# Sums of squares and low halves of weights on VectorE, and squares added beside the first up products, in a two-layer transformer kernel

## Chip, cores and metric

One Trainium2 chip, one core. The metric is device time in microseconds of one execution; the figure for the kernel before is the median of 3 runs. Engines are named TensorE (PE, with PEld for its weight loads), VectorE (DVE), ScalarE (ACT), GpSimd (POOL) and SyncE (SP).

## What is computed

Two layers over 512 tokens of width 1024 in float32. Each layer normalises its input, projects it (`w_in`), runs three groups of four attention heads (a forgetting one, a differential one with two maps a head, and a latent one), adds the output projection, normalises again and adds a feed-forward block with a causal convolution over three tokens:

```python
for i in range(DEPTH):
    h = rmsnorm(x, ln1_g[i]) @ w_in[i]
    ...
    x = x + jnp.concatenate([o_fox, o_diff, o_mla], axis=-1) @ w_o[i]
    up = causal_dwconv(rmsnorm(x, ln2_g[i]) @ w_up[i], conv_w[i], conv_b[i])
    g, u = up[..., :D_FF], up[..., D_FF:]
    x = x + (jax.nn.silu(g) * u) @ w_down[i]
return rmsnorm(x, final_g)
```

`rmsnorm(x, g)` is `x * rsqrt(mean(x * x) + 1e-6) * g`, the mean over the 1024 features of a token.

## The kernel before, in words

The residual lies transposed in eight tiles `x[0]` to `x[7]` (128 features by 512 tokens, float32; in the order listings `x_94` to `x_101`). Every operand of a product is split into a high half, the value rounded to fp32r, and a low half, the rest, and each product of two operands is three TensorE instructions (`mm3`): high by high, high by low, low by high. For an operand made on the chip (`split`; tiles named `a`), ScalarE writes the high half and VectorE the low one. For weights, `weights` hands out the next piece of a fixed list and keeps two pieces cut ahead: a load into one of three buffers `raw` on SyncE's queue, the high half `whi` by ScalarE, the low half `wlo` by VectorE, with four buffers of each. One kind is an exception (`ahead`): for the second piece of each of the 15 projection tiles of `w_fm` in a layer, GpSimd makes the low half.

A norm is not applied before its product. `Norm.halves` splits x times the gain, the product runs on that, and 1/rms is multiplied in behind it. The sum over features needs the squares: `Norm.square` has ScalarE square a tile and GpSimd add it to the tile `r` (seven sums for eight tiles). `Norm.sums` then lets TensorE sum over partitions (products with a column of ones), VectorE scales (`vn`), GpSimd takes the root (`rsn`), and `Norm.spread` spreads it over partitions by TensorE and copies it to `rb` by ScalarE.

The order of the work in a layer:

- Start: products with `w_fx`, tokens on the rows, in eight steps, one per x tile, of twelve products with 292 columns each. `Norm.ready` makes the halves and squares just ahead of each step, where they were not made by the layer before. In layer 0 all of this waits for the loads.
- The first two projection tiles (`fm`), during which the sums and 1/rms are made, then the values `w_dv`.
- The woven part: a planner (`Plan`, `weave`) counts times with its own costs per engine and decides when a step of the two heads in work goes next and when a filler (a projection tile, latent products, the output projection) goes instead. Its costs for a low half differ between VectorE and GpSimd, so the engine chosen changes the order.
- The rest of the output projection (`w_o2`): for each of eight x tiles six products, the sum into x on VectorE, the halves for the next norm, and its square.
- `ffn`: 22 pairs of up products (ft, gu), each 24 products of 512 columns; for each, VectorE multiplies by 1/rms (`u`), ScalarE and VectorE do the convolution (`w`), and a pair gives one tile of the hidden layer. In the first half eleven pairs are followed by eight down products, then the second half.

PSUM has three banks `mm` for products, two `sc` for scores, two `at` for transposes and sums, and one `o` for head outputs. In `ffn` the first up product (0, 0) goes before the sums, (0, 1) comes behind them with the spreading after its fourth step, and then VectorE begins with (0, 0).

An instruction's place on its engine is fixed when the program is built; it is mostly the order of the code, but an instruction that would wait can be passed by a later one. In the profile nearly every instruction has line 133 (the helper that the planner calls), and loads have 276, so rows are told apart by tile names.

Of the kernel before, what the change touches and what calls it, by code (L numbers as in the profile page):

```python
# [8 lines left out]
F32 = mybir.dt.float32  # L9
F32R = mybir.dt.float32r  # L10
AF = mybir.ActivationFunctionType
ALU = mybir.AluOpType
# [164 lines left out]
def build(tc, xT, cst, par, lamv, w_fm, w_dv, w_fx, w_uq, w_ukv, w_o, w_o2, w_up, w_dn, w_dt, fin, out):  # L177
# [4 lines left out]
    with ctx:  # L182
# [61 lines left out]
        def col(l, o, j=0):  # L244
            k = l * PL + o + j
            return par_sb[:, k:k + 1]
# [39 lines left out]
        def ahead():  # L286

            while state["cut"] < min(len(pieces), state["use"] + CUT_AHEAD):
                i, off, w = pieces[state["cut"]]
                while state["load"] < min(len(chunks), i + 3):  # L290
                    load()
                src = raws[i][:, off:off + w]
                if chunks[i][0].tensor.name == w_dt.tensor.name:
                    hi, lo = A(), A()
                else:
                    hi, lo = (plan.tile(v, CUT_BUFS, lp.tile([P, S], F32R, name=v, tag=v, bufs=CUT_BUFS))[:, :w] for v in ("whi", "wlo"))
                nc.scalar.activation(hi, src, AF.Copy)
                eng = nc.gpsimd if off and chunks[i][0].tensor.name == w_fm.tensor.name else nc.vector
                eng.tensor_tensor(out=lo, in0=src, in1=hi.bitcast(F32), op=ALU.subtract)
                ready.append((hi, lo))  # L300
                state["cut"] += 1

# [51 lines left out]
        class Norm:  # L354
# [5 lines left out]
            def halves(self, j):  # L360
                self.xs.append(split(x[j], scale=self.g(j)))

            def square(self, eng=None):
                j = self.squares
                self.squares += 1
                sq = R() if j == 0 else W()
                nc.scalar.activation(sq, x[j], AF.Square)
                if j == 0:
                    self.acc = sq
                else:  # L370
                    (eng or nc.gpsimd).tensor_tensor(out=self.acc, in0=self.acc, in1=sq, op=ALU.add)

            def ready(self, k):

                while len(self.xs) <= min(k, KD - 1):
                    self.halves(len(self.xs))
                    if len(self.xs) > 2:
                        self.square()

            def sums(self):  # L380
                while self.squares < KD:
                    self.square()
                self.rs = inv_rms(self.acc, D, "n")

            def spread(self):
# [139 lines left out]
        def attention(l, norm):  # L525
# [385 lines left out]
            for j in range(KD):  # L911
                ps = mm_ps()
                if j % 2 == 0:
                    hi, lo = weights(S, w_o2)
                for k in range(2):
                    c = slice((j % 2 * 2 + k) * P, (j % 2 * 2 + k + 1) * P)
                    mm3(ps, (hi[:, c], lo[:, c]), oT[6 + k], k == 0, k == 1)
                nc.vector.tensor_tensor(out=x[j], in0=ps, in1=x[j], op=ALU.add)
                nxt.halves(j)
                nxt.square()  # L920
            return nxt

        def ffn(l, norm):
            last = l == DEPTH - 1
            nxt = None if last else Norm(lambda j: col(l + 1, O_LN1, j))
            for half in range(2):
                hT = []
                for ft in range(half * HALF, (half + 1) * HALF):
                    y2, tiles = [], []

                    def raw(ps):
                        for k in range(KD):
                            if k % 4 == 0:
                                hi, lo = weights(S, w_up)
                            c = slice(k % 4 * P, (k % 4 + 1) * P)
                            mm3(ps, (hi[:, c], lo[:, c]), norm.xs[k], k == 0, k == KD - 1)
                            if ft == 0 and k == 3 and len(tiles) == 2:
                                norm.spread()

                    for gu in range(2):  # L940
                        if len(tiles) == gu:
                            tiles.append(mm_ps())
                            raw(tiles[-1])
                        if norm.rb is None:
                            norm.sums()
                            tiles.append(mm_ps())
                            raw(tiles[-1])
                        ps = tiles[gu]
                        a = U()
                        nc.vector.tensor_tensor(out=a, in0=ps, in1=norm.rb, op=ALU.mult)  # L950
                        y = W()
                        ch = gu * NFT + ft
                        nc.scalar.activation(y, a, AF.Identity, scale=col(l, O_CW, 88 + ch), bias=col(l, O_CB, ch))
                        for s_, o in ((1, 44), (2, 0)):
                            nc.vector.scalar_tensor_tensor(out=y[:, s_:], in0=a[:, :S - s_], scalar=col(l, O_CW, o + ch), in1=y[:, s_:], op0=ALU.mult, op1=ALU.add)
                        y2.append(y)
                    g, u = y2
                    nc.scalar.activation(g, g, AF.Silu)
                    nc.vector.tensor_tensor(out=u, in0=u, in1=g, op=ALU.mult)
                    hT.append(split(u, lo_eng=nc.gpsimd))  # L960
# [114 lines left out]
```

## Time and profile before

| what | us |
|---|---|
| median of 3 runs (1241.84 to 1244.34) | 1241.91 |
| the profiled execution | 1244.5 |
| its span, first to last instruction | 1242.7 |
| TensorE busy | 1210.6 |
| VectorE busy | 815.0 |
| ScalarE busy | 665.0 |
| GpSimd busy | 288.4 |

Busy times overlap. Products are pipelined: a row gives each some 0.39 us, while with 512 columns one starts about 0.2263 us after the other, so the distance of starts tells the rate. A number in brackets behind a row is the idle time of the engine before it and what ended it. A row with x3 is three instructions merged, with the time from the first's start to the last's end.

### The profile page before, as it was taken

To read this page: it belongs to the slowest core of one execution; us is meant where nothing else is said; L and a number is where in the kernel's file an instruction comes from. 1 tells how busy PE (TensorE), PEld (TensorE's weight loads), DVE (VectorE), ACT (ScalarE), POOL (GpSimd) and SP (SyncE) were. 2 spreads that over 40 slices of the span, in tenths; PEclk is the share of its full clock that TensorE was granted. 3 is DMA by queue.
4 is the path that set the end of the run, shared out by engine and by line. 5 is a ranking of instruction groups with operands and counts; after the bars stand their busy time and mean duration, and the time that the engine had idled before them with its cause. 6 is when DMAs were issued, how large, how long until landed. Compare 5 with 4: busy or idle time off the path is not lost.

```text
span 1242.7 us, 16525 instructions
## 1 busy us (share of the span) xinstructions
PE 1210.6 (97%) x5792; PEld 1010.2 (81%) x5792; DVE 815.0 (66%) x1632; ACT 665.0 (54%) x1323; POOL 288.4 (23%) x378
## 2 busy tenths in 40 slices
PE   6999999999999999999999999999999999999997
PEld 6878877878888888888898788788788888888886
DVE  5578778687665357665554887887767643666743
ACT  5477777565543245444454776875545422454524
POOL 4165353141110001111123636322211100011102
PEclk8999999999999999999999999999999999999999
DMA  5211110222222332223232111113222233222231
GB/s 208 94 68 69 56 51 26 95 78 95 99 92 83 98 119 102 86 86 94 86 115 82 69 65 44 48 38 102 86 102 98 68 101 124 87 100 102 86 118 68
DMA packets 34356, 108.33 MB, mean 87 GB/s; under 512 B 3808, under 2 KB 3936, under 8 KB 34272
## 3 DMA queue, kind: packets, MB, share of 16 engines
q1 hardware_dynamic: 33984, 106.81, 25.8%
q8 instruction: 45, 0.74, 0.2%
q10 hardware_dynamic: 288, 0.47, 0.1%
q14 instruction: 39, 0.32, 0.1%
HBM read 105.16 MB, written 2.10 MB: 86 GB/s over the span
## 4 chain that ended last, share of the span: by engine, by line
PE 86%; DVE 6%; POOL 3%; ACT 2%; issue 2%; DMA 0%; POOLq 0%; DVEq 0%; ACTq 0%
PE mm L133 75%; PE sc L133 5%; PE at L133 4%; DVE a L133 2%; PE o L133 2%; POOL rq L133 1%; POOL wlo L133 1%; DVE row L133 1%; DVE wlo L133 1%; DVE w L133 1%; ACT a L133 1%; DVE x L133 1%; POOL row L133 1%; ACT row L133 0%; ACT u L133 0%
## 5 line engine op out<-in xcount | busy, mean ns | idle before, releaser
L133 PE MATMUL mm<-a,whi 128*128 128x512 f32 x2800 | 872.5, 392 | 4.4 <-DVE a L133 4.4
L133 PEld LDWEIGHTS mm<-a,whi 128*128 128x128 f32 x2800 | 520.7, 188 | 108.7 <-DVE a L133 5.8
L133 PE MATMUL mm<-a,wlo 128*128 128x512 f32 x1400 | 546.1, 390 | 0.0
L133 ACT ACTIVATE whi<-raw 128x512 fp32r<-128x512 f32 (+3 forms) x426 | 248.9, 585 | 373.2 <-PE mm L133 323.9
L133 DVE TENSOR_TENSOR wlo<-raw,whi 128x512 fp32r<-128x512 f32 (+3 forms) x396 | 260.6, 660 | 132.2 <-ACT whi L133 127.2
L133 PEld LDWEIGHTS mm<-a,wlo 128*128 128x128 f32 x1400 | 262.9, 188 | 54.4
L133 POOL TENSOR_TENSOR a<-w,a 128x512 fp32r<-128x512 f32 x44 | 57.2, 1300 | 540.6 <-ACT a L133 521.4
L133 DVE SCALAR_TENSOR_TENSOR w<-u,par_sb,w 128x511 f32<-128x511 f32 (+1 forms) x176 | 132.1, 750 | 32.0 <-ACT w L133 28.9
L133 DVE TENSOR_TENSOR u<-mm,r 128x512 f32<-128x512 f32 x88 | 60.9, 692 | 107.3 <-PE mm L133 107.3
L133 ACT ACTIVATE a<-w 64x512 fp32r<-64x512 f32 (+1 forms) x124 | 78.4, 632 | 43.4 <-DVE w L133 41.8
L133 ACT ACTIVATE w<-u,par_sb 128x512 f32<-128x512 f32 x88 | 71.9, 817 | 33.1 <-DVE u L133 33.1
L133 POOL TENSOR_SCALAR row<-row,rsum 128x512 f32<-128x512 f32 (+1 forms) x96 | 58.0, 607 | 134.1 <-DVE rsum L133 132.4
L133 ACT ACTIVATE row<-row,nm 128x512 f32<-128x512 f32 (+1 forms) x96 | 53.8, 561 | 24.7 <-DVE nm L133 24.6
L133 PE MATMUL sc<-a 128*128 128x512 f32 (+7 forms) x288 | 66.9, 337 | 0.0
L133 DVE TENSOR_TENSOR x<-mm,x 128x512 f32<-128x512 f32 x64 | 43.9, 688 | 32.8 <-PE mm L133 32.5
L133 PE MATMUL mm<-whi,a 128*128 128x512 f32 (+2 forms) x176 | 56.1, 367 | 8.8 <-ACT whi L133 6.5
L133 POOL TENSOR_TENSOR r<-r,w 128x512 f32<-128x512 f32 x28 | 41.7, 1489 | 93.0 <-ACT w L133 92.0
L133 POOL TENSOR_TENSOR wlo<-raw,whi 128x512 fp32r<-128x512 f32 x30 | 39.9, 1329 | 82.2 <-ACT whi L133 82.1
L133 DVE TENSOR_TENSOR pl<-at,ph 128x128 fp32r<-128x128 f32 (+1 forms) x96 | 45.7, 484 | 7.8 <-ACT ph L133 7.0
L133 PEld LDWEIGHTS sc<-a 128*128 128x128 f32 (+1 forms) x288 | 46.2, 191 | 5.5 <-DVE nm L133 0.8
L133 ACT ACTIVATE ph<-at 128x128 fp32r<-128x128 f32 (+1 forms) x96 | 40.6, 433 | 15.7 <-PE at L133 11.3
L133 PE MATMUL at<-c_sb,row 128*128 128x128 f32 x240 | 43.0, 278 | 4.5 <-POOL row L133 1.9
(139 smaller groups left out, 1075.5 us busy)
## 6 DMA issues: line engine op xcount, KB each, us to landing
raw<-in_w_up SPq DMA_DIRECT2D x88, 512.0 KB, 3.2
raw<-in_w_fm SPq DMA_DIRECT2D x30, 512.0 KB, 3.2
raw<-in_w_dn SPq DMA_DIRECT2D x24, 384.0 KB, 3.0
raw<-in_w_dn SPq DMA_DIRECT2D x24, 320.0 KB, 2.8
raw<-in_w_o SPq DMA_DIRECT2D x16, 384.0 KB, 2.9
raw<-in_w_dv SPq DMA_DIRECT2D x8, 512.0 KB, 3.2
raw<-in_w_dn SPq DMA_DIRECT2D x8, 512.0 KB, 3.5
raw<-in_w_fx SPq DMA_DIRECT2D x8, 292.0 KB, 3.7
```

What stands on the lines that cost most here:

```text
L133: return real(*args, **kw)
```

## The change

Three things. The low halves of the projection weights are all made by VectorE. The sums of squares of all norms are made by VectorE, too. And in `ffn` the squares of the norm no longer belong to the output projection's loop but to the first up product (the first four after its fourth step, the rest after its last); (0, 0) and (0, 1) go to the two score banks, (1, 0) to a bank `mm`, and the sums come after the second step of (1, 0), the spreading after its seventh, all before VectorE begins with (0, 0). `made` keeps the products that are already there. The whole diff:

```diff
--- before.py
+++ after.py
@@ -295,8 +295,7 @@
                 else:
                     hi, lo = (plan.tile(v, CUT_BUFS, lp.tile([P, S], F32R, name=v, tag=v, bufs=CUT_BUFS))[:, :w] for v in ("whi", "wlo"))
                 nc.scalar.activation(hi, src, AF.Copy)
-                eng = nc.gpsimd if off and chunks[i][0].tensor.name == w_fm.tensor.name else nc.vector
-                eng.tensor_tensor(out=lo, in0=src, in1=hi.bitcast(F32), op=ALU.subtract)
+                nc.vector.tensor_tensor(out=lo, in0=src, in1=hi.bitcast(F32), op=ALU.subtract)
                 ready.append((hi, lo))
                 state["cut"] += 1
 
@@ -360,7 +359,7 @@
             def halves(self, j):
                 self.xs.append(split(x[j], scale=self.g(j)))
 
-            def square(self, eng=None):
+            def square(self):
                 j = self.squares
                 self.squares += 1
                 sq = R() if j == 0 else W()
@@ -368,7 +367,7 @@
                 if j == 0:
                     self.acc = sq
                 else:
-                    (eng or nc.gpsimd).tensor_tensor(out=self.acc, in0=self.acc, in1=sq, op=ALU.add)
+                    nc.vector.tensor_tensor(out=self.acc, in0=self.acc, in1=sq, op=ALU.add)
 
             def ready(self, k):
 
@@ -377,9 +376,12 @@
                     if len(self.xs) > 2:
                         self.square()
 
+            def squares_to(self, n):
+                while self.squares < n:
+                    self.square()
+
             def sums(self):
-                while self.squares < KD:
-                    self.square()
+                self.squares_to(KD)
                 self.rs = inv_rms(self.acc, D, "n")
 
             def spread(self):
@@ -917,35 +919,36 @@
                     mm3(ps, (hi[:, c], lo[:, c]), oT[6 + k], k == 0, k == 1)
                 nc.vector.tensor_tensor(out=x[j], in0=ps, in1=x[j], op=ALU.add)
                 nxt.halves(j)
-                nxt.square()
             return nxt
 
         def ffn(l, norm):
             last = l == DEPTH - 1
             nxt = None if last else Norm(lambda j: col(l + 1, O_LN1, j))
+            made = {}
+
+            def raw(ft, gu, bank=mm_ps, between={}):
+
+                ps = made[ft, gu] = bank()
+                for k in range(KD):
+                    if k % 4 == 0:
+                        hi, lo = weights(S, w_up)
+                    c = slice(k % 4 * P, (k % 4 + 1) * P)
+                    mm3(ps, (hi[:, c], lo[:, c]), norm.xs[k], k == 0, k == KD - 1)
+                    if k in between:
+                        between[k]()
+
+
+            raw(0, 0, sc_ps, {3: lambda: norm.squares_to(4), 7: lambda: norm.squares_to(KD)})
+            raw(0, 1, sc_ps)
+            raw(1, 0, mm_ps, {1: norm.sums, 6: norm.spread})
             for half in range(2):
                 hT = []
                 for ft in range(half * HALF, (half + 1) * HALF):
-                    y2, tiles = [], []
-
-                    def raw(ps):
-                        for k in range(KD):
-                            if k % 4 == 0:
-                                hi, lo = weights(S, w_up)
-                            c = slice(k % 4 * P, (k % 4 + 1) * P)
-                            mm3(ps, (hi[:, c], lo[:, c]), norm.xs[k], k == 0, k == KD - 1)
-                            if ft == 0 and k == 3 and len(tiles) == 2:
-                                norm.spread()
-
+                    y2 = []
                     for gu in range(2):
-                        if len(tiles) == gu:
-                            tiles.append(mm_ps())
-                            raw(tiles[-1])
-                        if norm.rb is None:
-                            norm.sums()
-                            tiles.append(mm_ps())
-                            raw(tiles[-1])
-                        ps = tiles[gu]
+                        if (ft, gu) not in made:
+                            raw(ft, gu)
+                        ps = made[ft, gu]
                         a = U()
                         nc.vector.tensor_tensor(out=a, in0=ps, in1=norm.rb, op=ALU.mult)
                         y = W()
```

VectorE at the start of layer 0 (`a<-x_97`: low half of an x tile; `wlo`: low halves of `w_fx`; `r<-r,w`: a sum of squares):

```order
 L133 SCALAR_TENSOR_TENSOR a<-x_97,par_sb,a 128x512
+L133 TENSOR_TENSOR r<-r,w 128x512
 L133 SCALAR_TENSOR_TENSOR a<-x_98,par_sb,a 128x512
 L133 TENSOR_TENSOR wlo<-raw,whi 128x292 x2
+L133 TENSOR_TENSOR r<-r,w 128x512
 L133 SCALAR_TENSOR_TENSOR a<-x_99,par_sb,a 128x512
+L133 TENSOR_TENSOR r<-r,w 128x512
 L133 SCALAR_TENSOR_TENSOR a<-x_100,par_sb,a 128x512
+L133 TENSOR_TENSOR r<-r,w 128x512
 L133 SCALAR_TENSOR_TENSOR a<-x_101,par_sb,a 128x512
+L133 TENSOR_TENSOR r<-r,w 128x512
 L133 TENSOR_TENSOR wlo<-raw,whi 128x292 x2
```

Five of the seven sums show here, each in front of a later low half; one more stands above, and the seventh below the last two low halves of `w_fx`.

VectorE at the entry of the feed-forward block of layer 0, the kernel before (`wlo`: low halves of `w_up`; `vn`: the scaled sum; `u<-mm,r`: an up product times 1/rms):

```order
L133 SCALAR_TENSOR_TENSOR a<-x_100,par_sb,a 128x512
L133 TENSOR_TENSOR wlo<-raw,whi 128x512
L133 SCALAR_TENSOR_TENSOR a<-x_101,par_sb,a 128x512
L133 TENSOR_TENSOR wlo<-raw,whi 128x512 x2
L133 TENSOR_SCALAR vn<-at 128x4
L133 TENSOR_TENSOR wlo<-raw,whi 128x512 x2
L133 TENSOR_TENSOR u<-mm,r 128x512
```

The same place in the changed kernel:

```order
L133 SCALAR_TENSOR_TENSOR a<-x_101,par_sb,a 128x512
L133 TENSOR_TENSOR r<-r,w 128x512
L133 TENSOR_TENSOR wlo<-raw,whi 128x512
L133 TENSOR_TENSOR r<-r,w 128x512
L133 TENSOR_TENSOR wlo<-raw,whi 128x512
L133 TENSOR_TENSOR r<-r,w 128x512
L133 TENSOR_TENSOR wlo<-raw,whi 128x512
L133 TENSOR_TENSOR r<-r,w 128x512 x3
L133 TENSOR_TENSOR wlo<-raw,whi 128x512
L133 TENSOR_TENSOR r<-r,w 128x512
L133 TENSOR_TENSOR wlo<-raw,whi 128x512
L133 TENSOR_SCALAR vn<-at 128x4
```

All seven sums stand behind the low half of the last x tile, and six low halves of weights, not three, come between that and `vn`. Behind `vn` follow a low half, two multiplications `u<-sc,r` from the score banks, a low half, four steps of the convolution, and `u<-mm,r` for (1, 0).

GpSimd in the woven part of layer 0 (`row`: scaling of a row of softmax; `a`: zeros for a key tile):

```order
 L133 TENSOR_SCALAR row_744<-row_744,rsum 128x512
 L133 TENSOR_SCALAR row_755<-row_755,rsum 128x384
-L133 TENSOR_TENSOR wlo<-raw,whi 128x512
 L133 MEMSET a 64x512
 L133 TENSOR_SCALAR row_782<-row_782,rsum 128x512
```

The low half that stood before the scaling of the next head's row is gone; the same happens 13 times in this part of each layer, and further down the order of the heads' steps and the fillers differs, too.

## Rows read from the trace of the kernel before

**Rows 1.** The page, part 1: busy us of each engine (share of the span), instructions.

```profile
PE 1210.6 (97%) x5792; PEld 1010.2 (81%) x5792; DVE 815.0 (66%) x1632; ACT 665.0 (54%) x1323; POOL 288.4 (23%) x378
```

**Rows 2.** List of waits on TensorE: total us, how many, the longest.

```profile
PE mm L133 <- DVE a L133: 4.8, 3, 2.2
PE mm L133 <- DVE wlo L133: 3.1, 1, 3.1
```

**Rows 3.** Timeline of TensorE, start: start us, us, what [idle before it].

```profile
16.91 0.30 PE L133 MATMUL mm<-wlo,a 128*128 128x292 f32 x1
17.60 0.53 PE L133 MATMUL mm<-whi,a 128*128 128x292 f32 x2 [0.40 <-DVE a L133]
...
18.91 0.29 PE L133 MATMUL sc<-whi,a 128*128 128x292 f32 x1
19.04 0.30 PE L133 MATMUL mm<-whi,a 128*128 128x292 f32 x1
22.41 0.61 PE L133 MATMUL mm<-wlo,a 128*128 128x292 f32 x1 [3.07 <-DVE wlo L133]
```

**Rows 4.** Busy us by stretch: PE, PEld, DVE, ACT, POOL, clock, DMA, GB/s.

```profile
22.40:28.20 5.80, 5.79 (x24) 5.79 (x25) 1.62 (x3) 0.63 (x1) 0.00 (x0) 0.50 0.51 183
```

**Rows 5.** Timeline of VectorE, start.

```profile
6.43 0.84 DVE L133 TENSOR_TENSOR wlo<-raw,whi 128x292 fp32r<-128x292 f32 x2
7.38 0.75 DVE L133 SCALAR_TENSOR_TENSOR a<-x,par_sb,a 128x512 fp32r<-128x512 f32 x1
...
15.76 5.15 DVE L133 SCALAR_TENSOR_TENSOR a<-x,par_sb,a 128x512 fp32r<-128x512 f32 x3
20.84 1.51 DVE L133 TENSOR_TENSOR wlo<-raw,whi 128x292 fp32r<-128x292 f32 x1
```

**Rows 6.** Timeline of ScalarE, start.

```profile
14.80 0.71 ACT L133 ACTIVATE a<-x,par_sb 128x512 fp32r<-128x512 f32 x1
```

**Rows 7.** Timeline of VectorE, entry of the feed-forward block of layer 0.

```profile
258.17 1.11 DVE L133 SCALAR_TENSOR_TENSOR a<-x,par_sb,a 128x512 fp32r<-128x512 f32 x1
...
264.32 1.78 DVE L133 TENSOR_TENSOR wlo<-raw,whi 128x512 fp32r<-128x512 f32 x1
266.02 1.74 DVE L133 SCALAR_TENSOR_TENSOR a<-x,par_sb,a 128x512 fp32r<-128x512 f32 x1
...
273.33 0.69 DVE L133 TENSOR_TENSOR u<-mm,r 128x512 f32<-128x512 f32 x1
...
279.10 0.69 DVE L133 TENSOR_TENSOR w<-w 128x512 f32<-128x512 f32 x1
279.71 0.69 DVE L133 TENSOR_TENSOR wlo<-raw,whi 128x512 fp32r<-128x512 f32 x1
```

**Rows 8.** Timeline of TensorE, the same entry.

```profile
265.22 0.39 PE L133 MATMUL mm<-a,whi 128*128 128x512 f32 x1
267.82 0.50 PE L133 MATMUL mm<-a,whi 128*128 128x512 f32 x1 [2.22 <-DVE a L133]
...
268.40 0.95 PE L133 MATMUL at<-ones,r 128*128 128x1 f32 x8
```

**Rows 9.** Groups of instructions by shape: count | busy us, mean ns | idle before.

```profile
L133 DVE TENSOR_TENSOR wlo<-raw,whi 128x512 fp32r<-128x512 f32 x248 | 174.2, 703 | 54.0 <-ACT whi L133 49.7 <-PE mm L133 2.7
...
L133 POOL TENSOR_TENSOR r<-r,w 128x512 f32<-128x512 f32 x28 | 41.7, 1489 | 93.0 <-ACT w L133 92.0
L133 POOL TENSOR_TENSOR wlo<-raw,whi 128x512 fp32r<-128x512 f32 x30 | 39.9, 1329 | 82.2 <-ACT whi L133 82.1
```

**Rows 10.** Chain of waits: start us, us, what.

```profile
272.62 351.71 PE mm L133 x1554
```

**Rows 11.** Busy us by stretch, woven attention of layer 0 (columns as rows 4).

```profile
60.00:160.00 100.00, 98.15 (x512) 82.55 (x511) 77.15 (x212) 73.22 (x172) 54.09 (x85) 1.00 0.19 64
160.00:180.00 20.00, 18.79 (x107) 15.78 (x105) 13.81 (x46) 12.43 (x38) 12.91 (x28) 1.00 0.18 60
180.00:200.00 20.00, 18.48 (x106) 14.78 (x103) 18.01 (x54) 17.50 (x50) 4.38 (x6) 1.00 0.08 25
```

## Prediction

> **What bounds the kernel now.** I read the page's table of engines first: TensorE is busy for 1210.6 of 1242.7 us [rows 1], so a change on another engine can only give back time in which TensorE stood still or ran slowly. The list of waits on TensorE comes next. Its two largest entries that VectorE ends are 4.8 us in three waits for the low halves of the norm's inputs (tile a) and 3.1 us in one wait for a weight's low half (wlo) [rows 2]. The timelines then place them. The wait for wlo and a short one for a (0.4 us) lie at the start of the program, the two others for a, 2.2 us each, where the feed-forward blocks begin.
>
> The start: TensorE's products of 292 columns follow each other at 0.13 us (18.91 to 19.04), but one at 16.91 is followed by the next at 17.60 and one at 19.04 by the next at 22.41 [rows 3], and from there until 28.2 the granted clock is 0.50, the lower of its two levels (1.2 GHz), with 24 products in 5.8 us, 0.24 us each [rows 4]. So the stall costs twice: its own time and the half clock behind it. VectorE is why: it needs 5.15 us for three low halves of x, of which one took 0.75 us before GpSimd began, and 1.51 us for the low half of 292 columns that TensorE waits for, where two of that size took 0.84 us earlier [rows 5]. In that stretch GpSimd adds the squares of the norm, 1489 ns each [rows 9].
>
> The entry of the feed-forward block: GpSimd adds squares again, and the last low halves on VectorE grow from 0.75 to 1.11, 1.78 and 1.74 us [rows 7]. TensorE starts a product at 265.22 and the next at 267.82 [rows 8]; 2.60 less the usual 0.2263 us (351.71 us for 1554 products [rows 10]) is 2.4 us lost. Layer 1 repeats it: 4.8 us in three waits are 2.2, 2.2 and 0.4 [rows 2]. Behind the entry the chain is pure TensorE for 351.71 us, so the rest of the feed-forward blocks has nothing to give.
>
> The third stage is the woven attention (60 to 246 us, and again in layer 1). TensorE idles 1.85 us of the 100 us from 60 to 160, 1.21 of the next 20, and 1.52 of the 20 from 180 [rows 11].
>
> **The change, part by part.** *Start of layer 0.* Seven sums of squares leave GpSimd for VectorE's queue, where six of them now stand ahead of the low half that TensorE waited for. Priced by the nearest sum of two SBUF tiles on VectorE, an instruction starts 0.61 us after the one before (279.10 to 279.71 [rows 7]). From 7.38 us on VectorE has seven low halves of x at 0.75, six sums at 0.61 and five low halves of 292 columns at 0.42 before it is done: 5.3 + 3.7 + 2.1 = 11.0 us, so 18.4 us, and about 17.8 us if neighbours overlap by the tenth that back-to-back starts show. ScalarE delivers the last input it needs at 15.5 [rows 6], one square later in the new order, so it is not the limit. TensorE, no longer held at 16.91 (0.69 less 0.13, so 0.56 us), reaches that point at 19.04 + 0.13 - 0.56 = 18.6. So the low half comes just in time, with 0.2 to 0.8 us in hand. If it is late by half a microsecond, that is less than the gap of 2.4 us at the entry, behind which the clock stayed at full. Gain: the two gaps, 0.56 and 3.37 - 0.13 = 3.24 us, and 24 products at 0.24 that become 0.13, 2.6 us: 6.4, taken as 6.5 because the first product of 512 columns began at half clock too. Bounds: 0 if VectorE is as late as now, 6.5 if the stall goes.
>
> *Entry of the feed-forward block, twice.* The squares stay on ScalarE at their place; the sums leave GpSimd and stand behind x_7's low half on VectorE. From 258.17 VectorE has five low halves of x, three sums into x and one low half of a weight in front of it: at most 5 x 0.75 + 4 x 0.69 = 6.5 us, so 264.7, and 263.9 with overlap. TensorE needs it at 265.45. Even alone VectorE is slower here than TensorE (about 1.8 us per x tile against six products, 1.36 us), but the first 22 products of the up projection need nothing new and cover the rest. So 2.4 us go, twice: 4.8 us. Bounds: 0 and 4.8.
>
> *What the sums then delay.* The first product starts at 265.22 - 21 x 0.2263 = 260.5 in both kernels. Before, the sums followed the first up projection product tile; now they follow 54 products, at 272.7. From there the old kernel took 4.9 us until VectorE used 1/rms (268.40 [rows 8] to 273.33 [rows 7]) with four groups of three products between; now five, so 5.6 us: VectorE starts on the up projection at 278.3 instead of 273.3, with three tiles waiting. Two of them lie in score banks, which nothing else wants before the next layer, and TensorE can fill two more mm banks until 288.9. VectorE frees the bank of (1, 0) after six instructions of 0.69 to 0.75 and a ScalarE answer of 0.8, by 284.9: no wait. The tightest point behind it is the second low half of (2, 1): eight more instructions, 5.8 us, so 290.7 at most, needed at 291.6. No cost, with 1 us in hand at full durations and 3 with overlap. The work that hides all this is those two tiles, 10.9 us of TensorE; were the cover gone, the 5.0 us by which 1/rms is later would show, per layer.
>
> *Low halves of projection weights.* 15 a layer go from GpSimd (1329 ns) to VectorE (703 ns) [rows 9]; 13 of them lie in the woven part, so GpSimd loses 17.3 us and VectorE gains 9.1 us, twelve of them in the 100 us where it is busy 77.15 us [rows 11]: about 86% instead of 77. The planner sees the new prices and moves the order of heads and filler products. For a gain: GpSimd's scaling of softmax rows no longer stands behind a 1.3 us low half. For a loss: every softmax step stands behind more on VectorE, and the new order spends filler products earlier, so that one more head is unfinished when the keys' products come. The nearest rows give the ends: all 3.06 us of idle time from 60 to 180 gone, or 9.1 us a layer added. Between them I take zero, by the stretch 60 to 160, where a VectorE at 77% left 1.85 us in 100.
>
> The squares that the down projection of layer 0 makes for layer 1 also move to VectorE (7 x 0.61 = 4.3 us). Behind 351.71 us without a gap, they cost nothing. No transfer is added or moved; SyncE's order is the same. GpSimd keeps only the roots, the rows, the biases and the feed-forward block's own low halves.
>
> **Sum.** -6.5 - 4.8 + 0 = -11.3 us. The profiled execution took 1244.5 us (span 1242.7), so it would take 1233.2. It lies 2.6 above the median of the runs, 1241.9; the forecast for the median is 1230.6 us. About 0.2%, 2.5 us, is what a measurement of this kernel can tell from no change.
>
> **Rivals.**
> 1. *The start still stalls and the clock still falls.* Six sums stand ahead of the low half and my margin is 0.2 to 0.8 us. Against it: gaps of 2.4 us did not lower the clock. If a gap remains and it falls, the half clock's 2.6 us and about 0.8 of a gap stay: 1234.0.
> 2. *VectorE's backlog after 1/rms reaches TensorE.* 1/rms comes 5 us later, and my margin at the second low half of (2, 1) is 1 to 3 us. It decides if VectorE's ten or so instructions take over 6.7 us instead of 5.8. Up to 5.0 us a layer: 1230.6 to 1240.6, 1235 in the middle.
> 3. *VectorE becomes the bound of the woven part; slower.* Its place is 60 to 180 us of each layer. If all 9.1 us a layer appear on TensorE, 18.2 - 11.3 = +6.9: 1248.8. If the 100 us become like 180 to 200 (18.01 of 20 us busy, 1.52 idle), 5 x 1.52 - 1.85 = 5.75 a layer: 1242.1. It turns the sign from 5.65 us a layer on. For it: the new order on VectorE and the earlier use of fillers. Against it: 86% is below the 90% of that row. The Trainium skill speaks for this rival: in "Perfetto Trace Analysis", Optimizing Scalar/DVE Operations, it says that with a saturated VectorE it may make sense to hand work to ScalarE or GpSimd, and this change does the reverse; by that rule the time would be that of this rival. The trace of before shows no saturation in that stretch, so I give it little. The same section adds that the two share a read port and that moving work between them might not help, which the stretched low halves [rows 5, 7] bear out.
> 4. *The change does not do what it says at the entry.* VectorE alone is slower than TensorE there; if x_7's low half is late without GpSimd too, the 4.8 us stay: 1235.4.
>
> **How the numbers follow.** The forecast has 0.60, rival 1 0.10, rival 2 0.09, rival 3 0.13 (a half of it near 1242, 0.05 slower), rival 4 0.08. The likeliest alone spans 1225 (woven idle gone in part) to 1234. The range reaches over rivals 1 and 4 and most of 2: 1225 to 1239. Faster by over 0.2% means below 1239.4: the forecast, rivals 1 and 4 and most of 2, 0.87. Same 0.07, slower 0.06.
>
> **What would show it.** In the profile after: no gap over 1 us on TensorE before 30 us and a granted clock of 1.00 from 12 us on, with the first products of 512 columns near 21.6 instead of 28.2; low halves of x at 0.75 us with no 1.1 to 1.8; no wait of mm for a at the entries; VectorE's sums at about 0.69 us; its first product with 1/rms about 18 us after the block's first product, and TensorE without a gap behind it; VectorE near 86% from 60 to 160 with some 2 us of idle TensorE. What would make it wrong: waits of at and sc for VectorE's pl, nm and row in the woven part that sum to over 5 us a layer, or a second fall of the clock.

## The result, and the profile after

The changed kernel takes 1224.83 us (median of 4 runs, 1224.06 to 1225.15) against 1241.88 for the kernel before beside it (4 runs): a ratio of 0.9857, 95% interval 0.984 to 0.9874, so 17 us faster. The direction was forecast, the size was not: 1224.83 is 5.8 us below the forecast of 1230.6 and 0.2 below the lower end of the range. The profiled execution's span went from 1242.7 to 1222.8 us, 19.9 less. That is more than the 17 us between the medians, because executions of the kernel before vary, and their clock with them (25 of them beside the experiments took from 1239.7 us, at a mean granted clock of 0.999, to 1247.3, at 0.993), and the profiled one, at 0.996, took 2.6 us more than the median.

The page's busy times after the change; GpSimd falls from 288.4 to 208.9 us, VectorE rises by 7.3 only [rows 1]:

```profile
PE 1205.2 (99%) x5792; PEld 1006.9 (82%) x5792; DVE 822.3 (67%) x1690; ACT 661.8 (54%) x1323; POOL 208.9 (17%) x320
```

The list of waits on TensorE after (total, how many, longest). Both entries of [rows 2], for a and for wlo, are gone:

```profile
PE mm L133 <- ACT whi L133: 6.0, 1, 6.0
PE sc L133 <- DVE nm L133: 1.5, 2, 0.8
PE at L133 <- POOL row L133: 0.9, 2, 0.4
PE at L133 <- DVE pl L133: 0.8, 2, 0.4
```

To find where the 19.9 us of span went, I take the starts of instructions that both programs have in the same place: the first product of 512 columns, the first up product of each layer, and the spreading of 1/rms at layer 1's start. TensorE's timeline before (the second row is the first up product, found by its place behind the output projection):

```profile
28.17 0.51 PE L133 MATMUL mm<-a,whi 128*128 128x512 f32 x1
...
260.46 0.61 PE L133 MATMUL mm<-a,whi 128*128 128x512 f32 x2
...
641.20 0.49 PE L133 MATMUL at<-c_sb,rsn 128*128 128x128 f32 x3
...
868.36 0.62 PE L133 MATMUL mm<-a,whi 128*128 128x512 f32 x2
```

And after, where the up products go to score banks:

```profile
20.94 0.63 PE L133 MATMUL mm<-a,whi 128*128 128x512 f32 x2
...
249.27 0.62 PE L133 MATMUL sc<-a,whi 128*128 128x512 f32 x2
...
627.55 0.60 PE L133 MATMUL at<-c_sb,rsn 128*128 128x128 f32 x4
...
850.93 0.62 PE L133 MATMUL sc<-a,whi 128*128 128x512 f32 x2
```

The differences of these starts, with the start of the span and its end, make five stages:

| stage | before | after | change | forecast |
|---|---|---|---|---|
| A: start, to the first product of 512 columns | 28.17 | 20.94 | -7.23 | -6.5 |
| B: projections and woven part of layer 0, to its first up product | 232.29 | 228.33 | -3.96 | 0 |
| C: feed-forward block of layer 0 and layer 1's start | 380.74 | 378.28 | -2.46 | -2.4 |
| D: projections and woven part of layer 1 | 227.16 | 223.38 | -3.78 | 0 |
| E: feed-forward block of layer 1, to the end | 374.34 | 371.87 | -2.47 | -2.4 |

Three of the five are as forecast, within 0.8 us. B and D, where I took zero, hold 7.7 us: most of the 8.6 by which these 19.9 exceed the forecast of 11.3. By the medians the forecast lacks 5.8. Which stage gains less in a median execution than here was not traced; A, with the half clock of the kernel before, is the likeliest.

### The profile page after: what moved, and what is told of

It reads as the page before. It is cut to its first block, busy times and chain, and to the rows that moved or that the text cites. A ratio compares the mean times of both kernels' runs of the same rounds, so it can differ in the third digit from the quotient of the medians.

```text
span 1222.8 us, 16493 instructions
## 1 busy us (share of the span) xinstructions
PE 1205.2 (99%) x5792; PEld 1006.9 (82%) x5792; DVE 822.3 (67%) x1690; ACT 661.8 (54%) x1323; POOL 208.9 (17%) x320
## 4 chain that ended last, share of the span: by engine, by line
PE 94%; DVE 2%; ACT 2%; POOL 1%; issue 0%; DMA 0%; POOLq 0%; ACTq 0%; DVEq 0%
PE mm L133 80%; PE sc L133 8%; PE at L133 4%; PE o L133 3%; DVE w L133 1%; ACT u L133 1%; POOL b L133 0%; ACT row L133 0%; POOL row L133 0%; DVE a L133 0%; DVE row L133 0%; DMA par_sb<-in_par 0%; ACT a L133 0%; POOL rsd L133 0%; ACT w L133 0%
## 5 line engine op out<-in xcount | busy, mean ns | idle before, releaser
L133 PE MATMUL mm<-a,whi 128*128 128x512 f32 x2736 | 851.0, 392 | 0.0
L133 PEld LDWEIGHTS mm<-a,whi 128*128 128x128 f32 x2736 | 508.6, 188 | 101.5 <-ACT a L133 0.4
L133 PE MATMUL mm<-a,wlo 128*128 128x512 f32 x1368 | 533.1, 390 | 0.0
L133 DVE TENSOR_TENSOR wlo<-raw,whi 128x512 fp32r<-128x512 f32 (+3 forms) x426 | 273.0, 642 | 131.5 <-ACT whi L133 126.6
L133 PEld LDWEIGHTS mm<-a,wlo 128*128 128x128 f32 x1368 | 256.9, 188 | 53.5
L133 DVE SCALAR_TENSOR_TENSOR w<-u,par_sb,w 128x510 f32<-128x510 f32 (+1 forms) x176 | 133.1, 761 | 27.7 <-ACT w L133 24.9
L133 DVE TENSOR_TENSOR u<-mm,r 128x512 f32<-128x512 f32 x84 | 58.0, 691 | 98.7 <-PE mm L133 98.7
L133 POOL TENSOR_SCALAR b<-r,cum 128x128 f32<-128x128 f32 (+2 forms) x56 | 28.8, 527 | 74.4 <-ACT r L133 54.4
L133 PEld LDWEIGHTS mm<-whi,a 128*128 128x128 f32 x176 | 33.1, 194 | 9.1 <-ACT whi L133 6.0
```

The source lines that it names most:

```text
L133: return real(*args, **kw)
```

## The experiments

The table gives the same five stages for ten of the runs, each from its profiled execution. Differences between experiments are read from it and from the medians; the two agree within 1 us, except for the kernel before. A ratio is against the kernel before as it ran beside that group (medians 1241.4 to 1243.9), so ratios of different groups compare less closely than medians. TensorE's first product starts between 5.6 and 6.5 us, as the first load lands, so A varies by some 0.9 us without a cause in the kernel; where two programs have the same work there, B to D repeat within 0.1 us and E within 0.4.

| run | A | B | C | D | E | span | median |
|---|---|---|---|---|---|---|---|
| before | 28.2 | 232.3 | 380.7 | 227.2 | 374.3 | 1242.7 | 1241.88 |
| after | 20.9 | 228.3 | 378.3 | 223.4 | 371.9 | 1222.8 | 1224.83 |
| 1: low halves alone | 25.8 | 228.3 | 380.7 | 223.3 | 374.3 | 1232.5 | 1233.6 |
| 2: low halves back | 20.7 | 232.0 | 378.3 | 227.0 | 371.8 | 1229.8 | 1231.8 |
| 3: new engine, old order | 21.3 | 229.6 | 378.3 | 224.4 | 371.9 | 1225.4 | 1227.18 |
| 4: old engine, new order | 20.6 | 230.7 | 378.3 | 225.7 | 371.5 | 1226.8 | 1229.34 |
| 5: sums back on GpSimd | 25.5 | 228.3 | 380.8 | 223.4 | 374.4 | 1232.4 | 1234.17 |
| 6: old order of the entry | 21.5 | 230.1 | 379.1 | 225.0 | 372.7 | 1228.3 | 1229.89 |
| 7: idle copy on GpSimd | 20.8 | 233.3 | 378.3 | 227.9 | 371.5 | 1231.8 | 1233.95 |
| 8: idle power on GpSimd | 20.0 | 231.9 | 378.3 | 226.4 | 371.9 | 1228.5 | 1231.0 |

**Runs 1 and 2: is it the low halves?** Run 1 is the kernel before with the first part of the change alone, run 2 the changed kernel without it. The edit of run 1 (run 2 is its reverse):

```diff
-                eng = nc.gpsimd if off and chunks[i][0].tensor.name == w_fm.tensor.name else nc.vector
-                eng.tensor_tensor(out=lo, in0=src, in1=hi.bitcast(F32), op=ALU.subtract)
+                nc.vector.tensor_tensor(out=lo, in0=src, in1=hi.bitcast(F32), op=ALU.subtract)
```

> The kernel before with one edit of the change: all low halves of projection weights on VectorE; sums of squares and the feed-forward entry as before. If the 7.4 us that the woven parts lost come from these low halves, whichever way, 1234.5 us (1233 to 1236), with the stall at the start (3 us and the half clock) and the two waits of 2.2 us at the entries still there. If the woven part gained from the earlier start or from the squares, it stays at 1241.9.

> The changed kernel with the second low halves of projection weights back on GpSimd. By the first theory above 1232.2 us (1224.8 + 7.4), with a clean start and clean entries; by the other 1224.8.

Run 1 took 1233.6 us, ratio 0.9924 (0.9894 to 0.9954); run 2 1231.8, ratio 0.9903 (0.9879 to 0.9928), 7.0 us above the changed kernel. In the table the part lies in B and D: 232.0 to 232.3 and 227.0 to 227.2 with these low halves on GpSimd, 228.3 and 223.3 to 223.4 without, whatever was done to the sums. (In run 1, A falls by 2.4 us too, 0.3 of it the first load: together with GpSimd's sums its low halves lengthen the start, while in run 2, without the sums, they don't.)

**Runs 3 and 4: the engine, or the order that the planner made of it?** In run 3 VectorE makes the low halves, and the planner is told GpSimd's price; in run 4 GpSimd makes them and the planner is told VectorE's.

```diff
+                eng = Engine(plan, "POOL", tc.nc.vector) if off and chunks[i][0].tensor.name == w_fm.tensor.name else nc.vector
+                eng.tensor_tensor(out=lo, in0=src, in1=hi.bitcast(F32), op=ALU.subtract)
```

(run 3; run 4 has `"DVE", tc.nc.gpsimd`)

> The changed kernel, the low halves on VectorE, but the planner is told that GpSimd makes them, so the order of heads and fillers on TensorE is that of the kernel before. Theory A (the engine: 1.3 us low halves no longer stand before rows on GpSimd): near 1224.8, at most 1226.5. Theory B (the order: the planner arranged heads and fillers better): near 1232.2, at least 1230.5.

> The mirror image: GpSimd makes the second low halves, but the planner is told that VectorE does, so the order on TensorE is that of the changed kernel but for a few rows. Theory A: near 1232.2 or worse, since rows wait behind low halves that the plan does not know of. Theory B: near 1224.8, at most 1226.5.

Run 3 took 1227.18 us, ratio 0.9865 (0.984 to 0.989), run 4 1229.34, ratio 0.9885 (0.9855 to 0.9915). Neither theory holds alone. From run 2, the engine gives back 4.6 us and the order 2.5, and 4.6 + 2.5 is the 7.0 between run 2 and the changed kernel: two effects that add.

The traces show the engine's part at one place of layer 0. VectorE, run 2, subtracts two low halves of 64 partitions (start, duration):

```profile
66.73 2.33 DVE L133 TENSOR_TENSOR a<-w,a 64x512 fp32r<-64x512 f32 x2
69.10 0.22 DVE L133 RECIPROCAL rsum<-ssum 128x1 f32<-128x1 f32 x2
```

while GpSimd, run 2, makes the low half of a weight, zeros a tile and then waits for rsum before it scales rows:

```profile
66.52 1.28 POOL L133 TENSOR_TENSOR wlo<-raw,whi 128x512 fp32r<-128x512 f32 x1
67.86 0.52 POOL L133 MEMSET a<- 64x512 f32 x1
69.43 1.25 POOL L133 TENSOR_SCALAR row<-row,rsum 128x512 f32<-128x512 f32 x2 [1.05 <-DVE rsum L133]
```

VectorE in run 3, at the same instructions:

```profile
66.81 1.41 DVE L133 TENSOR_TENSOR a<-w,a 64x512 fp32r<-64x512 f32 x2
68.25 0.16 DVE L133 RECIPROCAL rsum<-ssum 128x1 f32<-128x1 f32 x1
```

The pair takes 2.33 us beside GpSimd and 1.41 without, so the reciprocals and the scaled rows behind them come 0.85 us sooner (69.10 to 68.25, and on GpSimd 69.43 to 68.58). On TensorE a wait of 0.90 us for VectorE at 69.91 is gone in run 3, and the transposes that wait for a scaled row start at 73.59 instead of 74.06. Here it was not GpSimd's queue that held the row (GpSimd idled 1.05 us, waiting for rsum) but VectorE, slowed by GpSimd.

**Runs 7 and 8: the queue, or the slowing?** The changed kernel, plus one instruction on GpSimd beside every second low half of a projection weight, whose output nobody reads. The order on the other engines stays as it is. Run 7 repeats the low half into a spare tile; run 8 takes a power of six columns instead, about as long with hardly any data.

```diff
                 nc.vector.tensor_tensor(out=lo, in0=src, in1=hi.bitcast(F32), op=ALU.subtract)
+                if off and chunks[i][0].tensor.name == w_fm.tensor.name:
+                    tc.nc.gpsimd.tensor_tensor(out=spare, in0=src, in1=hi.bitcast(F32), op=ALU.subtract)
```

(run 7, without the line that makes `spare`; in run 8 `in0=c_sb[:, C_ONE:C_ONE + 6], in1=hi[:, :6].bitcast(F32), op=ALU.pow`)

> The changed kernel, in which GpSimd also makes the second low half of each projection tile, into a tile that nobody reads; the order on all other engines is that of the changed kernel. So GpSimd's work is back without anyone waiting for its result. If GpSimd's sum of two SBUF tiles stretches VectorE's neighbours (the pair of low halves at 64 partitions took 2.33 us beside one and 1.41 without), the engine part comes back, 4.6 us: 1229.4. If GpSimd's queue is what hurt (softmax rows behind 1.3 us), the same 4.6: 1229.4. If the lateness of the low half itself was what hurt, nothing comes back: 1225.

> As the run with the idle copy, but at the same places GpSimd takes a power of 6 columns instead, for which the rows of 1 and 4 columns (0.54 and 1.02 us) let one expect about 1.35 us: the same time in GpSimd's queue with hardly any bytes moved. The output is not read by anyone. If VectorE's stretching is what hurt, nothing is lost: 1225. If GpSimd's queue is what hurt, as much is lost as in the run with the idle copy: 1229.4.

Run 7 took 1233.95 us, ratio 0.9919 (0.9901 to 0.9938): 9.1 above the changed kernel, twice what either theory expected. Run 8 took 1231.0, ratio 0.9896 (0.9877 to 0.9914): 6.2 above. GpSimd's instruction took nearly the same time in both, some 15% more than the low half had taken in the kernel before (1329 ns [rows 9]; groups by line: busy us, mean ns; run 7):

```profile
L301 POOL TENSOR_TENSOR spare<-raw,whi 128x512 fp32r<-128x512 f32 x30 | 45.8, 1527 | 139.4 <-ACT whi L133 125.0 <-DVE a L133 7.4 <-issue 5.0
```

and run 8:

```profile
L301 POOL TENSOR_TENSOR spare<-c_sb,whi 128x6 f32<-128x6 f32 x30 | 46.7, 1558 | 141.4 <-ACT whi L133 141.3
```

The pair of low halves on VectorE at the place shown above, run 7:

```profile
66.83 2.48 DVE L133 TENSOR_TENSOR a<-w,a 64x512 fp32r<-64x512 f32 x2
```

and run 8:

```profile
66.19 1.49 DVE L133 TENSOR_TENSOR a<-w,a 64x512 fp32r<-64x512 f32 x2
```

So the power leaves VectorE as it is (1.49 us) and still costs 6.2 us: that is GpSimd's queue, where softmax rows wait. TensorE's waits for such rows, 0.9 us in the changed kernel, are in run 8

```profile
PE at L133 <- POOL row L133: 3.6, 5, 1.3
```

which is about half of the 5.7 us of span; the rest is put down to the queue because VectorE's durations stayed. The copy costs 2.95 us more: that is the slowing, by which the groups of VectorE's 64-partition low halves and of its weights' low halves grow from 27.9 and 273.0 us in the changed kernel to 31.4 and 280.4 in run 7; in run 8 they are 27.9 and 273.7. (The copy also reads `raw`, and 13 loads waited for that, 18.3 us in all; TensorE waited for no weight behind the first load, so this rival to the slowing shows no cost there.) Both theories were right and both prices too low. I had expected the engine's 4.6 us to come back, but that is a difference of two costs: in the move GpSimd loses work and VectorE gains it. Run 4 and run 7 both have the low half on GpSimd, and their orders are nearly the same; in run 7 VectorE makes it as well, and it is 4.6 us slower. So the 4.5 us between run 4 and the changed kernel are the remainder of 9.1 us that GpSimd's work cost and 4.6 that VectorE's now costs (an estimate, since the two orders differ in a few rows and the copy takes some 15% longer than the low half).

**Runs 5 and 6: the sums, and their place.** Run 5 is the changed kernel with the sums of squares on GpSimd. Run 6 is the kernel before with everything on VectorE, but the squares still in the output projection's loop.

```diff
-                    nc.vector.tensor_tensor(out=self.acc, in0=self.acc, in1=sq, op=ALU.add)
+                    nc.gpsimd.tensor_tensor(out=self.acc, in0=self.acc, in1=sq, op=ALU.add)
```

(run 5; run 6 is the kernel before with the sums on VectorE, as in the line with the minus, and with the edit of run 1)

> The changed kernel with one thing undone: the sums of squares are GpSimd's again; the new order of the feed-forward block's entry and VectorE's low halves stay. If the engine of the sums is what the start was about, the start's 7.2 us of span come back (gap at the low half of 292 columns, granted clock 0.50 behind it) and the entries stay free of gaps, since the last x tile's low half now stands ahead of all sums: 1224.8 + 7 = 1232. If the entries also hung on the engine, GpSimd's sums beside the first up products stretch VectorE's low halves and make 1/rms late, and 2.4 us for each entry come on top: 1237. If neither, 1225.

> The kernel before with all low halves and all sums of squares on VectorE, and with the old order of the feed-forward block's entry: squares and sums inside the output projection's loop. Theory that moving the squares behind the low halves was needed: five sums of 0.61 us stand ahead of the last x tile's low half on VectorE, which had 1 to 1.5 us in hand without them, so about 1.6 to 2.2 us are lost at each of the two entries: 1228 to 1229.3. Rival, that taking GpSimd off is enough, since nothing is stretched any more: no gap at the entries, 1225. Start and woven part as in the changed kernel.

Run 5 took 1234.17 us, ratio 0.9919 (0.99 to 0.9938): 9.3 above the changed kernel, near neither figure that I gave, because it loses in both places: 4.5 us in A and 2.5 in each of C and E. The new place of the squares in the program does not keep them back; ScalarE made them when it was free, and GpSimd summed six in one stretch from 250.46. VectorE beside it:

```profile
255.93 0.68 DVE L133 TENSOR_TENSOR x<-mm,x 128x512 f32<-128x512 f32 x1
256.54 1.18 DVE L133 SCALAR_TENSOR_TENSOR a<-x,par_sb,a 128x512 fp32r<-128x512 f32 x1
257.64 1.78 DVE L133 TENSOR_TENSOR wlo<-raw,whi 128x512 fp32r<-128x512 f32 x1
259.34 1.74 DVE L133 SCALAR_TENSOR_TENSOR a<-x,par_sb,a 128x512 fp32r<-128x512 f32 x1
```

and TensorE, which waits for the last:

```profile
261.14 0.50 PE L133 MATMUL sc<-a,whi 128*128 128x512 f32 x1 [2.21 <-DVE a L133]
```

Those are the durations and the gap of the kernel before [rows 7, 8], in the new order.

Run 6 took 1229.89 us, ratio 0.9885 (0.9863 to 0.9907): 5.1 above the changed kernel, 0.6 above the upper figure of the first theory. A is free of its stall, here and in run 2, so taking the sums off GpSimd is enough for the start. (The 0.6 us by which run 6's A exceeds the changed kernel's lie ahead of 12 us, where its products stay 0.24 us apart until 11.75, not 10.34.) But the entries lose as much as before, 2.5 us each (part of it lies ahead of the first up product there, so in B and D), without any slowing, since sums now stand ahead of x's sums and low halves on VectorE's own queue (run 6):

```profile
249.47 0.75 DVE L133 SCALAR_TENSOR_TENSOR a<-x,par_sb,a 128x512 fp32r<-128x512 f32 x1
250.14 0.69 DVE L133 TENSOR_TENSOR r<-r,w 128x512 f32<-128x512 f32 x1
250.74 0.68 DVE L133 TENSOR_TENSOR x<-mm,x 128x512 f32<-128x512 f32 x1
```

TensorE, run 6, waits for that sum to have a bank free, and later for the root:

```profile
251.57 0.70 PE L133 MATMUL mm<-a,whi 128*128 128x512 f32 x2 [1.38 <-DVE x L133]
...
261.40 0.65 PE L133 MATMUL at<-c_sb,rsn 128*128 128x128 f32 x4 [0.45 <-POOL rsn L133]
```

At the entry, then, either half of the change alone gives nothing: off GpSimd in the old place loses 2.5 us an entry, in the new place on GpSimd 2.5 too; together the loss is gone.

**Runs 9 to 12: can it be pushed further?** Run 9 puts the key tiles' zeros on VectorE and moves one product in the last rows; run 10 moves a key copy from ScalarE to GpSimd; runs 11 and 12 change the planner's patience, that is, how long after its inputs a step of a head may go.

```diff
-                    nc.gpsimd.memset(lo[other].bitcast(F32), 0.0)
+                    nc.vector.memset(lo[other].bitcast(F32), 0.0)
```

(run 9, the first of its two parts; run 10: `nc.gpsimd.tensor_copy(k[other], k[own].bitcast(F32))`; runs 11, 12: `SLACK` -1.0, -2.0 instead of -1.5)

> The changed kernel with the zeros of the key tiles (10 in the woven part of each layer, 0.52 us each on GpSimd) on VectorE, and in the last rows the product with the final gain behind the sum of squares instead of ahead of it. If time in GpSimd's queue is dear at the rate of the run with the idle power (some 20 us of it cost 3.1 us a layer), 5.2 us less give back 0.8 us a layer; the last rows give 0.6 us, since the sum of squares waited for 0.6 us of VectorE: 1224.8 - 2.2 = 1222.6. If VectorE's time is as dear as GpSimd's, only the last rows gain: 1224.2.

> The changed kernel with the second high half of each key tile (10 in the woven part of each layer) copied by GpSimd instead of ScalarE, to see if what moved to another engine must come off GpSimd, or if any relief helps: the largest gap left (0.93 us at 108) stands behind 2.58 us of such copies on ScalarE. If GpSimd's queue is the dear one, the copies cost at least as much as the idle power, about 0.15 us for each us: if one takes 1 us, +1.5 us a layer less the 0.9 us of the gap: 1226. If relief of ScalarE weighs more: 1223.

> The changed kernel with the planner's SLACK at -1.0 instead of -1.5: a step of a head may go 0.5 us sooner after its inputs. It tells how much of the order's share (2.5 us of 7 in the runs that set order and engine apart) is luck of one order. If any order of the planner does about as well, within 1.5 us of 1224.8; if the order of the changed kernel is a lucky one, 1227 or more.

> The same with SLACK at -2.0: a step of a head goes 0.5 us later after its inputs, so that there is more room for late rows, and fillers are used up sooner. Within 1.5 us of 1224.8 if the order matters little; 1227 or more if the fillers run out before the last heads.

None beats the changed kernel. Run 9: 1225.62 us, ratio 0.9863 (0.984 to 0.9887), no difference that can be told; neither the zeros nor the last rows gave anything, and its B and D are 0.4 to 0.5 us longer. Run 10: 1228.06, ratio 0.9878 (0.9847 to 0.9908); the gap it aimed at went, and a larger wait came, for GpSimd itself:

```profile
PE sc L133 <- POOL a L133: 3.4, 4, 1.1
```

Behind these waits the granted clock was 0.50 from 174 to 177 us, and again from 778 to 781, so part of run 10's loss is the clock; its fastest execution, at a mean clock of 0.999, took 1225.77, only 0.9 above the changed kernel.

Run 11: 1236.81, ratio 0.9947 (0.9928 to 0.9966), its runs spread from 1231.43 (mean clock 0.996) to 1237.39 (0.992); run 12: 1231.68, ratio 0.9913 (0.989 to 0.9937). Half a microsecond of patience either way costs at least 6.6 us. In layer 1 of both profiled executions, a stretch at a granted clock of 0.50 (770.5 to 773.8 and 764.3 to 767.7 us) has a part in it; in layer 0, where the clock stayed at 1.00, B is still 2.9 and 3.1 us longer than in the changed kernel. So the order of the woven part is worth several microseconds by itself, and that it moved 2.5 us the right way with the new prices is, by these two runs, not something to count on.

## Why the prediction was right or wrong

*Start: right.* Forecast -6.5; A gives -7.23, of which 0.43 is that TensorE's first product started at 6.02 instead of 6.45. The walk along VectorE's queue held to a few tenths. VectorE after the change:

```profile
15.56 0.74 DVE L133 SCALAR_TENSOR_TENSOR a<-x,par_sb,a 128x512 fp32r<-128x512 f32 x1
16.22 0.68 DVE L133 TENSOR_TENSOR r<-r,w 128x512 f32<-128x512 f32 x1
16.82 0.83 DVE L133 TENSOR_TENSOR wlo<-raw,whi 128x292 fp32r<-128x292 f32 x2
```

Low halves of x take 0.74 us where they took 5.15 for three [rows 5], a sum starts 0.60 us ahead of the next instruction, as priced, and the pair of low halves ends at 17.65, and the first product with one of them starts at 17.88: at least 0.2 us in hand, the lower end of what I gave. The clock, after, in the stretch of [rows 4]:

```profile
22.40:28.20 5.80, 5.80 (x33) 4.96 (x32) 3.27 (x15) 3.02 (x7) 1.14 (x2) 1.00 0.35 112
```

So rival 1 did not come, and runs 2 and 6 show that moving the sums suffices here. One reading was incomplete: beside the low half of 292 columns that took 1.51 us at 20.84 [rows 5], GpSimd had finished its sums and made a low half of a projection weight (the kernel before):

```profile
20.33 1.71 POOL L133 TENSOR_TENSOR wlo<-raw,whi 128x512 fp32r<-128x512 f32 x1
```

Without it, in run 1, the longest wait there is 2.0 us instead of 3.1, and A is 2.4 us shorter. So the stall had two causes, one behind the other, and the forecast named the first.

*Entry: right, and for the reasons given.* The change is -2.46 and -2.47 against -2.4 each. The last low halves of x are back at 0.75 us, and the step needed both the engine (run 5) and the place behind x_7's low half (run 6). Rival 4, that VectorE alone is too slow there, did not come, but run 6 shows a loss of the same size for the old place, with the sums ahead of it.

*The delayed 1/rms: right.* VectorE uses 1/rms first at 267.13, 17.9 us after the first up product; the forecast was 278.3 less 260.5, 17.8. (The sum that frees the bank of (1, 0) by 284.9 is one of eight VectorE instructions, not six; its result stands.) The chain of waits after (start, duration, how many):

```profile
249.43 10.88 PE sc L133 x48
260.31 1.36 PE mm L133 x6
262.46 3.57 PE mm L133 x15
266.46 344.23 PE mm L133 x1521
```

Behind the spreading it is TensorE without a gap, as before [rows 10], so rival 2 did not come.

*Low halves of projection weights: wrong.* The step that failed is "Between them I take zero". It measured -3.96 and -3.78 us, 7.7 in all, and even the lower end that I gave, -3.06 a layer, was too narrow. By that end the sum comes to 1224.5, and the range stopped short of it, at 1225. Two things were wrong in the step.

First, the end. I bounded the gain by TensorE's idle time from 60 to 180 us in the busy times by stretch [rows 11]. Over the whole of stage B (layer 0) TensorE idled 5.02 us in the kernel before, 1.92 after, so 3.10 of the 3.96 is idle time; the other 0.86 is less time that the profile counts as busy (227.27 to 226.41). The list of waits of the kernel before shows where the idle time was: these entries of it lie in the woven parts (the kernel before):

```profile
PE at L133 <- DVE pl L133: 2.9, 4, 0.9
PE mm L133 <- DVE v L133: 1.9, 2, 1.0
PE at L133 <- POOL row L133: 1.9, 4, 0.7
PE at L133 <- ACT u L133: 1.4, 2, 0.7
PE at L133 <- DVE row L133: 0.8, 2, 0.4
```

Together 8.9 us, more than half of which is gone after the change, where sc for nm, at for row and at for pl make 3.2. I named the waits of at and sc only as what would show a loss, and did not read how much they could give back.

Second, the middle. I set 17.3 us less on GpSimd against 9.1 more on VectorE and took zero between the two ends. The runs price them apart: GpSimd's queue 6.2 us, its slowing of VectorE 3.0 (runs 7 and 8), less VectorE's added work, about 4.6 (an estimate from runs 4 and 7), and the planner's order gives 2.5 more. The first two are somewhat high for the move itself, as the instructions of runs 7 and 8 were the longer ones; what the runs show without that estimate is that the engine gives 4.6 and the order 2.5. The slowing was in the forecast at the start and at the entries, and I did not carry it into the woven part, where the same pairing of engines occurs: the same row of GpSimd that I quoted for its 1329 ns [rows 9] also stretched VectorE.

*Rival 3, VectorE as the bound: did not come.* The stretches of [rows 11] after the change:

```profile
60.00:160.00 100.00, 98.68 (x515) 83.53 (x515) 81.55 (x231) 73.46 (x175) 47.87 (x89) 1.00 0.18 60
160.00:180.00 20.00, 19.99 (x115) 16.28 (x115) 17.61 (x51) 17.32 (x47) 5.54 (x11) 1.00 0.16 54
180.00:200.00 20.00, 19.40 (x123) 15.58 (x123) 17.41 (x66) 16.36 (x59) 6.39 (x11) 1.00 0.12 41
```

VectorE is busy for 81.55 of 100 us, not 86. Part of its 77.15 before was slowing: between runs 2 and 3, which differ in the engine but hardly in the order, it goes from 76.68 to 82.20, 5.5 more where the low halves alone were priced at 8.4. TensorE idles 1.32, 0.01 and 0.60 us.

## What to carry to other kernels

When work moves between VectorE and GpSimd, price three things, not one: the receiver's added time, the queue of the engine that is relieved (who waits behind it for a result), and what the slower engine does to its neighbour while it runs. Bound a possible gain by all the idle time and all the waits of the stage, not by those of one stretch of it; even that left out 0.9 of 3.96 us here. And where a planner's costs decide the order, an edit of those costs is an edit of the order, worth several microseconds of either sign here; give that term a width of its own.

## What the hardware showed beside that

The slowing is selective. Beside GpSimd's sums in run 5, VectorE's low halves, which read two tiles from SBUF, took 1.18 to 1.78 us, and `x<-mm,x`, which reads one of its two from PSUM, 0.68 as ever. A power of six columns on GpSimd (run 8) left VectorE's low halves as they were, 27.9 and 273.7 us against 27.9 and 273.0. The Trainium skill, "GPSIMD Engine Reference", Key points, says that GpSimd shares its SBUF interfaces with VectorE and contends with instructions that have two SBUF inputs; the trace agrees, with these numbers.

The clock does not follow the length of a gap alone. In the kernel before, 3.07 us of waiting at 19 to 22 us [rows 3] were followed by a granted clock of 0.50 until 28.2 [rows 4]; in run 5, 2.01 us of waiting at the same place were followed by this (stretch, busy us of PE, PEld, DVE, ACT, POOL, clock, DMA, GB/s):

```profile
22.00:28.00 6.00, 6.00 (x34) 5.69 (x34) 1.80 (x4) 1.26 (x2) 0.00 (x0) 0.78 0.54 179
```

and 2.21 us of waiting at its entry, ended at 261.14, by this:

```profile
258.00:264.00 6.00, 3.79 (x17) 2.79 (x16) 4.98 (x5) 1.05 (x2) 2.46 (x2) 1.00 0.22 59
264.00:270.00 6.00, 6.00 (x32) 5.10 (x31) 1.55 (x3) 1.26 (x2) 0.23 (x1) 1.00 0.39 132
```

In run 10 waits of 1.06 and 0.64 us, with the start of a product between them, were enough for 0.50 from 174 us on. What tells these places apart was not tried.
